# Thirty-two modulation sums on VectorE, moved behind the steps of a layer norm

## The chip, the core and the metric

The kernel runs on one core of a Trainium2 chip. The metric is device time in microseconds (us) for one execution. All times and rows here are of the kernel before.

The engines are TensorE (PE, with its weight loads PEld), VectorE (DVE), ScalarE (ACT), GpSimd (POOL) and SyncE (SP), which issues all DMAs of this kernel. Each engine works through its own instructions in a fixed order; an instruction that must wait holds up all that stands behind it on its engine.

## What is computed

One layer of a streaming encoder over 1024 tokens of width 1024, in float32. Cut to what matters here:

```python
mod = silu(c) @ w_ada + b_ada                     # 6 x 1024 numbers, one set for all tokens
shift1, scale1, gate1, shift2, scale2, gate2 = split(mod, 6)
h = rms_norm(x, norm1_g) * (1 + scale1) + shift1
z = h @ w_in                                      # query latent | key/value latent | rope key | conv | gates
q = rms_norm(z_q, ...) @ w_uq                     # attention branch
kv = rms_norm(z_kv, ...) @ w_ukv
u = causal_depthwise_conv(glu(z_glu), ...)        # convolution branch, 512 channels
u = silu(layer_norm(u, conv_ln_g, conv_ln_b))
x = x + gate1 * ((g_a * y_a + g_b * y_b) @ w_out)
x = x + gate2 * (relu((rms_norm(x) * (1 + scale2) + shift2) @ w_ff1) ** 2 @ w_ff2)
```

Of `mod`, the first third (shift1, scale1) is needed at once. The other 4 x 1024 numbers (gate1, shift2, scale2, gate2) are needed only after the attention.

## The kernel before

**Numbers in pairs.** A float32 matrix product is made of three products of rounded halves: `split` writes a rounded copy `hi` on ScalarE (L110) and the remainder `lo` on VectorE or GpSimd (L116). Names that end in hi/h and lo/l are such halves.

**The modulation sums.** One sum (`ada`, L276) multiplies a 128 x 1024 tile `wada` of w_ada by silu(c) and adds up each row: 128 numbers of `mod`, one column. It is two rows in a trace (the product and the reading of the accumulator). Sixteen sums belong to shift1 and scale1 and are done at the start. The 32 later ones, S1 to S32 in what follows, fill `mods`. Their tiles are loaded by SyncE (L271) into six buffers in turn, so the load for S7 waits until S1 has been done.

**The stretch of the change.** TensorE multiplies h by w_in, one 128-column tile after another, 48 products of 128x512 for a tile (`z` in the rows; `gate`, `z_tile`). Each tile writes two of four PSUM banks, which ScalarE (or VectorE) has to read out before a later tile may use them. The weights of a tile are loaded into `wraw` (L131), then split: `whi` on ScalarE, `wlo` on GpSimd. In order: ten gate tiles, the query latent in two tiles (`zr0`, `zr1`), the key/value latent (`zr2`), gate tile 10, the rope key (`zkr`), gate tiles 11 and 12. Beside this VectorE, ScalarE and GpSimd make the depthwise convolution (`conv`, L440 to L459) and then its layer norm (L488 to L514):

- `lnsum`: the four channel tiles `acc0` to `acc3` are added; split into `sh`, `sl`; TensorE adds up over channels with a column of ones (16 products of 128x2, "the statistics"); VectorE makes the mean `mu`; TensorE spreads it over the partitions by transposes (`spread`, L235); VectorE subtracts it (L498).
- `lnvar`: ScalarE squares, VectorE adds the squares (L504), again `sh`, `sl`, statistics, then 1/sqrt (`rln`, through a square root on ScalarE, L211), the spread and the products (L509).
- `sg`: a sigmoid on ScalarE (L511), gain and offset on GpSimd (L512), the last product on VectorE (L513), and a store to `cd` (L514). The tiles are read back much later.

Then comes the norm of the query latent (`latent_norm`, L592): squares of `zr0`, `zr1` into `lsq` and `lsq1` on ScalarE (L595, L598), sums of them on VectorE (L599), halves `lsh`, `lsl`, statistics on TensorE, `rl`, its spread, `zr` (L609), halves `zh`, `zl`. The same again for the key/value latent. `lsq` lies where the layer norm's `acc` tiles lay, so it waits for their stores.

**What sets the order.** The program is written step by step; the framework arranges the instructions of every engine by its own estimate of when each could run. `tc.issue_after(x)` only says that what stands in its block comes behind x on x's engine. Before the change all 32 sums stand in one such block behind `after`, the last instruction of the convolution, and are written behind the whole layer norm (L515). In the trace they run from 209 us to 275 us, between the steps of the layer norm.

Of the kernel before, what the change touches and what calls it, by code (L numbers as in the profile page):

```python
# [8 lines left out]
F32 = mybir.dt.float32  # L9
# [3 lines left out]
ALU = mybir.AluOpType  # L13
# [6 lines left out]
P = 128  # L20
C = 512
KD = D // P
# [55 lines left out]
def block_kernel(ctx: ExitStack, tc: tile.TileContext, a: dict, out: bass.AP):  # L78
# [23 lines left out]
    def cs(c):  # L102
        return slice(c * C, (c + 1) * C)
# [9 lines left out]

    def split(hi, lo, src, hi_eng, lo_eng):
        copy(hi_eng, hi, src)
        lo_eng.tensor_tensor(lo, src, hi.bitcast(F32), ALU.subtract)  # L116

    def mm(o, l, r, start, stop):
        nc.tensor.matmul(o, l, r, start=start, stop=stop)  # L119
# [79 lines left out]
    def stat_cols(src_hi, src_lo, blocks, off=0, st=None):  # L199

        st = bank("c") if st is None else st
        for b in range(blocks):
            o = st[:, 2 * b:2 * b + 2]
            mm(o, src_hi[:, blk(off + b)], ones, True, False)
            mm(o, src_lo[:, blk(off + b)], ones, False, True)
        return st[:, 0:2 * blocks].rearrange("p (b two) -> p b two", two=2)[:, :, 0]
# [10 lines left out]
    def rsqrt(pool, ssq, n, shape, name):  # L217

        ms = pool.tile(shape, F32, name=name + "_ms", bufs=1)
        r = pool.tile(shape, F32, name=name, bufs=1)  # L220
        t = pool.tile(shape, F32, name=name + "_t", bufs=1)
        nc.vector.tensor_scalar(ms, ssq, 1.0 / n, EPS, ALU.mult, ALU.add)
        last_rsqrt[0] = refined(r, ms, t)
        return r

    def spread(col, outs=None):

        return spread_rows(lambda t: col[:, t:t + 1].broadcast_to([P, P]), col.shape[1], outs)
# [187 lines left out]
    with tc.tile_pool(name="cv", bufs=1, **right) as cv:  # L416
        accs = [cv.tile([P, S], F32, name=f"acc{i}") for i in range(KC)]

        def tmp(name, dt=F32):
            return cv.tile([P, S], dt, name=name, tag="tmp", bufs=5)  # L420
# [57 lines left out]
        phase.close()  # L478
        phase.enter_context(psum(z=4, c=2, q=2))

        def sum_cols(src):
            sh_ = tmp("sh", F32R)
            sl_ = tmp("sl", F32R)
            for c in range(2):
                split(sh_[:, cs(c)], sl_[:, cs(c)], src[:, cs(c)], nc.scalar, nc.vector)
            return stat_cols(sh_, sl_, NB)

        s_ = tmp("lnsum")  # L488
        nc.gpsimd.tensor_tensor(s_, accs[0], accs[1], ALU.add)
        nc.vector.tensor_tensor(s_, s_, accs[2], ALU.add)  # L490
        nc.vector.tensor_tensor(s_, s_, accs[3], ALU.add)
        mu = cv.tile([P, NB], F32, name="mu")
        nc.vector.tensor_scalar(mu, sum_cols(s_), 1.0 / CH, None, ALU.mult)
        rb = spread(mu)
        vs = tmp("lnvar")
        for i in range(KC):
            for c in range(2):
# [3 lines left out]
            else:  # L501
                sq = tmp("lnsq")
                nc.scalar.activation(sq, accs[i], AF.Square)
                nc.vector.tensor_tensor(vs, vs, sq, ALU.add)  # L504
        r = rsqrt(cv, sum_cols(vs), CH, [P, NB], "rln")
        rb = spread(r)
        for i in range(KC):
            for c in range(2):
                nc.vector.tensor_tensor(accs[i][:, cs(c)], accs[i][:, cs(c)], rb[c], ALU.mult)  # L509
            sg = tmp("sg")  # L510
            nc.scalar.activation(sg, accs[i], AF.Sigmoid, scale=v("ln_g", i), bias=v("ln_b", i))  # L511
            nc.gpsimd.tensor_scalar(accs[i], accs[i], v("ln_g", i), v("ln_b", i), ALU.mult, ALU.add)  # L512
            nc.vector.tensor_tensor(accs[i], accs[i], sg, ALU.mult)  # L513
            nc.sync.dma_start(c_d[i], accs[i])  # L514
        with tc.issue_after(after.ins):  # L515
            for i in range(2, 6):
                for k in range(KD):
                    ada(mods[i - 2][:, k:k + 1], i * KD + k)
        nc.vector.scalar_tensor_tensor(amp2, scale2, 1.0, v("g2", 0, KD), ALU.add, ALU.mult)
        adap.close()  # L520

# [796 lines left out]
```

## Time and profile before

| | |
|---|---|
| median of 3 runs | 1380.77 us (1376.42 to 1384.38) |
| profiled execution | 1386.99 us |
| its span | 1385.2 us, mean granted clock of TensorE 0.988 |
| PE busy | 1325.0 us (96%) |
| DVE busy | 992.1 us (72%) |
| ACT busy | 686.0 us (50%) |
| POOL busy | 415.7 us (30%) |

How to read it: the span runs from the first to the last instruction of the profiled execution. That execution is 6.2 us longer than the median. TensorE is busy nearly throughout, so a wait on another engine matters only where TensorE then has nothing to do, or where its granted clock falls.

### The profile page before, as it was taken

To read this page: it belongs to the slowest core of one execution; us is meant where nothing else is said; L and a number is where in the kernel's file an instruction comes from. 1 tells how busy PE (TensorE), PEld (TensorE's weight loads), DVE (VectorE), ACT (ScalarE), POOL (GpSimd) and SP (SyncE) were. 2 spreads that over 40 slices of the span, in tenths; PEclk is the share of its full clock that TensorE was granted. 3 is DMA by queue.
4 is the path that set the end of the run, shared out by engine and by line. 5 is a ranking of instruction groups with operands and counts; after the bars stand their busy time and mean duration, and the time that the engine had idled before them with its cause. 6 is when DMAs were issued, how large, how long until landed. Compare 5 with 4: busy or idle time off the path is not lost.

```text
span 1385.2 us, 17860 instructions
## 1 busy us (share of the span) xinstructions
PE 1325.0 (96%) x6104; PEld 1079.5 (78%) x6104; DVE 992.1 (72%) x1526; ACT 686.0 (50%) x1115; POOL 415.7 (30%) x289
## 2 busy tenths in 40 slices
PE   4999999999999999999999999998999999999998
PEld 3787888777777888877787888876888888887787
DVE  6679997954347888877556899777773469857854
ACT  6545412245657777753354864434454444443343
POOL 0069822243566676435000004333433000000000
PEclk9999999999999999999999999999999999999999
DMA  9601227631285333137636565665557678633442
GB/s 345 238 31 61 92 99 288 251 109 71 85 296 204 104 120 102 69 119 231 188 131 220 175 228 198 206 210 186 194 185 256 207 229 289 200 95 92 146 128 76
DMA packets 105115, 233.93 MB, mean 169 GB/s; under 512 B 12352, under 2 KB 12608, under 8 KB 105024
## 3 DMA queue, kind: packets, MB, share of 16 engines
q1 hardware_dynamic: 105024, 232.79, 49.9%
q8 instruction: 48, 0.79, 0.2%
q14 instruction: 43, 0.35, 0.1%
HBM read 169.83 MB, written 62.91 MB: 168 GB/s over the span
## 4 chain that ended last, share of the span: by engine, by line
PE 61%; DVE 14%; DMA 10%; issue 5%; ACT 4%; POOL 4%; SPq 1%; DVEq 0%; POOLq 0%; ACTq 0%
PE z L119 49%; PE s L119 3%; DMA wraw<-in_w_ff 3%; PE t L119 3%; POOL accp L450 2%; PE v L119 2%; PE t L799 2%; DVE wada L276 1%; DMA gat<-sg 1%; DVE big L998 1%; DMA wada<-in_w_ada 1%; DVE u L1028 1%; DVE wlo L116 1%; PE x L119 1%; DVE wraw L999 1%
## 5 line engine op out<-in xcount | busy, mean ns | idle before, releaser
L119 PE MATMUL z<-hhi,whi 128*128 128x512 f32 x384 | 153.1, 399 | 2.9 <-ACT sg L406 2.9
L119 PE MATMUL z<-hhi,wlo 128*128 128x512 f32 x384 | 152.3, 398 | 1.5 <-POOL wlo L116 1.5
L119 PE MATMUL z<-hlo,whi 128*128 128x512 f32 x384 | 152.6, 397 | 0.0
L1053 POOL TENSOR_TENSOR t<-u 128x512 f32<-128x512 f32 x16 | 21.6, 1348 | 298.2 <-DVE wy L986 171.4
L457 DVE SCALAR_TENSOR_TENSOR k<-u,vec,k 128x1024 f32<-128x1024 f32 x84 | 101.0, 1283 | 0.0
L110 ACT ACTIVATE whi<-wraw 128x1024 fp32r<-128x1024 f32 x71 | 74.4, 1048 | 41.4 <-PE z L119 33.9
L116 POOL TENSOR_TENSOR wlo<-wraw,whi 128x1024 fp32r<-128x1024 f32 (+1 forms) x23 | 56.1, 2440 | 122.8 <-ACT whi L110 122.8
L119 PEld LDWEIGHTS z<-hhi,whi 128*128 128x128 f32 x384 | 72.6, 189 | 21.5 <-ACT sg L406 3.5
L119 PEld LDWEIGHTS z<-hhi,wlo 128*128 128x128 f32 x384 | 72.4, 189 | 19.8 <-POOL wlo L116 1.9
L119 PEld LDWEIGHTS z<-hlo,whi 128*128 128x128 f32 x384 | 72.6, 189 | 17.8
L1019 ACT ACTIVATE u<-u 128x512 f32<-128x512 f32 x64 | 40.1, 631 | 85.4 <-DVE u L1028 81.7
L116 DVE TENSOR_TENSOR wlo<-wraw,whi 128x1024 fp32r<-128x1024 f32 x48 | 63.4, 1321 | 24.6 <-ACT whi L110 24.5
L276 DVE CUSTOM_DVE_ANT_0 wada<-wada,c_act,vec 128x1024 f32<-128x1024 f32 x48 | 68.0, 1455 | 10.6 <-DMA wada<-in_w_ada 7.3
L1028 DVE TENSOR_TENSOR u<-z,u 128x512 f32<-128x512 f32 x80 | 53.9, 686 | 23.5 <-DMA fdT<-u 11.2
L450 POOL TENSOR_TENSOR accp<-accp,prc 128x1024 f32<-128x1024 f32 x28 | 69.3, 2479 | 1.4
L119 PE MATMUL z<-ghT,hi 128*128 128x512 f32 x160 | 62.7, 392 | 0.3 <-DVE u L1028 0.3
L119 PE MATMUL z<-ghT,lo 128*128 128x512 f32 x160 | 62.5, 391 | 0.0
L119 PE MATMUL z<-glT,hi 128*128 128x512 f32 x160 | 62.4, 390 | 0.0
L119 PE MATMUL z<-l_whi,h_whi 128*128 128x512 f32 x148 | 58.8, 398 | 3.2 <-DVE l_whi L116 3.2
L119 PE MATMUL z<-l_wraw,h_wraw 128*128 128x512 f32 x152 | 59.6, 392 | 0.0
L119 PE MATMUL z<-h_wraw,l_wraw 128*128 128x512 f32 x152 | 59.2, 389 | 0.0
L119 PE MATMUL z<-h_whi,l_whi 128*128 128x512 f32 x148 | 58.6, 396 | 0.0
(365 smaller groups left out, 3859.6 us busy)
## 6 DMA issues: line engine op xcount, KB each, us to landing
wada<-in_w_ada SPq DMA_DIRECT2D x48, 512.0 KB, 6.2
wraw<-in_w_ff SPq DMA_DIRECT2D x32, 512.0 KB, 4.4
fraw<-fdT SPq DMA_DIRECT2D x64, 256.0 KB, 2.6
wraw<-in_w_in SPq DMA_DIRECT2D x24, 512.0 KB, 3.6
fd<-u SPq DMA_DIRECT2D x48, 256.0 KB, 3.4
fdT<-t SPq DMA_DIRECT2D x48, 256.0 KB, 4.1
fraw<-fd SPq DMA_DIRECT2D x48, 256.0 KB, 2.7
w<-in_w_ff SPq DMA_DIRECT2D x48, 256.0 KB, 3.8
```

What stands on the lines that cost most here:

```text
L110: eng.activation(o, i, AF.Copy)
L116: lo_eng.tensor_tensor(lo, src, hi.bitcast(F32), ALU.subtract)
L119: nc.tensor.matmul(o, l, r, start=start, stop=stop)
L276: nc.vector.tensor_tensor_reduce(out=w, in0=w, in1=c_act, scale=1.0, scalar=v("b_ada", j), op0=ALU.mult, op1=ALU.add, accum_out=dst,)
L450: nc.gpsimd.tensor_tensor(accp, accp, pr, ALU.add)
L457: nc.vector.scalar_tensor_tensor(t, u[:, j:j + S], w(j), t, ALU.mult, ALU.add)
L799: nc.tensor.transpose(pt[:, blk(n)], probs[q - i + 1][:, blk(kb)], ident)
L998: nc.vector.tensor_tensor(q[:, cs(0)], p[:, cs(0)], q[:, cs(0)], ALU.subtract)
L999: nc.vector.tensor_tensor(p[:, cs(1)], p[:, cs(1)], y[:, cs(1)], ALU.subtract)
L1019: nc.scalar.activation(f, f, AF.Relu)
L1028: last_sum[0] = nc.vector.tensor_tensor(t, x, y, ALU.add)
L1053: nc.gpsimd.tensor_tensor(t3, f22, f12, ALU.subtract)
```

## The change

The 32 sums are no longer in one block. A list `others` holds them; `more(n, step)` takes the next n and writes them behind the instruction `step`, and `split` now returns its last instruction so that it can serve as one. One sum stands behind the convolution, 3 behind the `sl` of the mean, 2 behind `mu`, 2 behind the `sl` of the variance, 1 behind the 1/sqrt, 2 behind the last product with it, and the other 21 behind the layer norm's last product. Nothing that is computed changes.

```diff
-        lo_eng.tensor_tensor(lo, src, hi.bitcast(F32), ALU.subtract)
+        return lo_eng.tensor_tensor(lo, src, hi.bitcast(F32), ALU.subtract)
...
+        others = [(i, k) for i in range(2, 6) for k in range(KD)]
+
+        def more(n, step):
+            with tc.issue_after(step.ins):
+                for _ in range(min(n, len(others))):
+                    i, k = others.pop(0)
+                    ada(mods[i - 2][:, k:k + 1], i * KD + k)
...
-            return stat_cols(sh_, sl_, NB)
+            st = stat_cols(sh_, sl_, NB)
+            more(n, o)
+            return st
...
+        more(1, after)
...
-        nc.vector.tensor_scalar(mu, sum_cols(s_), 1.0 / CH, None, ALU.mult)
+        o = nc.vector.tensor_scalar(mu, sum_cols(s_, 3), 1.0 / CH, None, ALU.mult)
         rb = spread(mu)
+        more(2, o)
...
-        r = rsqrt(cv, sum_cols(vs), CH, [P, NB], "rln")
+        r = rsqrt(cv, sum_cols(vs, 2), CH, [P, NB], "rln")
         rb = spread(r)
+        more(1, last_rsqrt[0])
...
+            if i == KC - 1:
+                more(2, o)
...
-        with tc.issue_after(after.ins):
-            for i in range(2, 6):
-                for k in range(KD):
-                    ada(mods[i - 2][:, k:k + 1], i * KD + k)
+        more(len(others), o)
```

How many of the 32 sums stand ahead of a step in VectorE's order, and what lies between the steps in TensorE's order:

| step on VectorE | sums ahead, before | now | on TensorE | before | now |
|---|---|---|---|---|---|
| last addition of `lnsum` | 6 | 1 | products of the gate tiles ahead of the mean's statistics | same place | same place |
| first subtraction of the mean | 21 | 6 | products from the mean's statistics to its spread | 20 | 19 |
| last addition of `lnvar` | 31 | 6 | from that spread to the variance's statistics | 115 | 63 |
| first product with `rln` | 32 | 9 | from those to the spread of `rln` (and 4 or 2 inside them) | 26 | 26 |
| last product of the layer norm | 32 | 11 | from there to the first statistic of the query latent | 98 | 120 |
| first addition of `lsq` | 32 | 17 | | | |
| `lsl` of the query latent | 32 | 20 | | | |
| `zr` of the query latent | 32 | 28 | | | |

The orders of the engines differ from the mean's spread up to the first part of the attention (some 250 to 500 us in the trace), and are the same behind it.

VectorE at the variance, before: the additions of the squares with sums between them (`mod5` is the last column group, gate2).

```order
L504 TENSOR_TENSOR lnvar_1820<-lnvar_1820,lnsq_1831 128x1024
L276 ISA wada_1993,mod5_78<-wada_1993,c_act_102,vec_63 128x1024
L276 ISA mod5_78 128x1
L276 ISA wada_1996,mod5_78<-wada_1996,c_act_102,vec_63 128x1024
L276 ISA mod5_78 128x1
L276 ISA wada_1999,mod5_78<-wada_1999,c_act_102,vec_63 128x1024
L276 ISA mod5_78 128x1
L504 TENSOR_TENSOR lnvar_1820<-lnvar_1820,lnsq_1836 128x1024
```

VectorE at the variance, now:

```order
L517 TENSOR_TENSOR lnvar_1838<-lnvar_1838,lnsq_1844 128x1024
L517 TENSOR_TENSOR lnvar_1838<-lnvar_1838,lnsq_1849 128x1024
L517 TENSOR_TENSOR lnvar_1838<-lnvar_1838,lnsq_1854 128x1024
L116 TENSOR_TENSOR sl_1858<-lnvar_1838,sh_1857 128x512 x2
L276 ISA wada_1880,mod2_75<-wada_1880,c_act_102,vec_63 128x1024
```

The additions and `sl` now stand in a row; the next sum (S7) comes behind them.

VectorE at the norm of the query latent, before: nothing stands between its steps.

```order
L513 TENSOR_TENSOR acc3_690<-acc3_690,sg_1904 128x1024
L599 TENSOR_TENSOR lsq_2144<-lsq_2144,lsq1_2146 128x512
L599 TENSOR_TENSOR lsq_2144<-lsq_2144,lsq1_2150 128x512
L116 TENSOR_TENSOR lsl_2154<-lsq_2144,lsh_2153 128x512 x2
L222 TENSOR_SCALAR rl_ms_2176<-c_2159 128x8
```

The same place now, from the first addition on; ahead of it, behind the layer norm's last product, stand S12 to S17.

```order
L612 TENSOR_TENSOR lsq_2144<-lsq_2144,lsq1_2146 128x512
L276 ISA wada_1960,mod4_77<-wada_1960,c_act_102,vec_63 128x1024
L276 ISA mod4_77 128x1
L612 TENSOR_TENSOR lsq_2144<-lsq_2144,lsq1_2150 128x512
L276 ISA wada_1963,mod4_77<-wada_1963,c_act_102,vec_63 128x1024
L276 ISA mod4_77 128x1
L276 ISA wada_1966,mod4_77<-wada_1966,c_act_102,vec_63 128x1024
L276 ISA mod4_77 128x1
L116 TENSOR_TENSOR lsl_2154<-lsq_2144,lsh_2153 128x512 x2
```

Nine sums have come ahead of `lsl`, three of them between its own steps.

ScalarE behind the query latent's 1/sqrt, before (`sg_2528` and `sg_2531` read gate tile 11 out of its banks, `zh0` and `zh1` are halves of the query latent, `lsq_2269` the squares of the key/value latent):

```order
L211 ACTIVATE rl_2177<-rl_ms_2176 128x8
L406 ACT_TABLE_LOAD
L406 ACTIVATE sg_2528<-z_2478 128x512
L110 ACTIVATE whi_2536<-wraw_2534 128x1024
L406 ACTIVATE sg_2531<-z_2479 128x512
L110 ACTIVATE zh0_2195<-zr0_2025 128x512
```

ScalarE at the same place now:

```order
L211 ACTIVATE rl_2177<-rl_ms_2176 128x8
L110 ACTIVATE zh0_2195<-zr0_2025 128x512
L110 ACTIVATE zh1_2203<-zr1_2026 128x512
L110 ACTIVATE zh0_2195<-zr0_2025 128x512
L608 ACTIVATE lsq_2269<-zr2_2027 128x512 x2
L110 ACTIVATE zh1_2203<-zr1_2026 128x512
L406 ACT_TABLE_LOAD
L406 ACTIVATE sg_2528<-z_2478 128x512
```

The halves and the squares have come ahead of the sigmoid of gate tile 11. A second change of this kind stands at the end of the key/value latent's norm: there `whi`, a table load and a sigmoid of gate tile 12 have come between the square root and the halves `zh2`.

## Rows read from the trace of the kernel before

**Rows 1.** The page: busy time of the first engine, and the chain by engine.

```profile
PE 1325.0 (96%) x6104; PEld 1079.5 (78%) x6104; DVE 992.1 (72%) x1526; ACT 686.0 (50%) x1115; POOL 415.7 (30%) x289
PE 61%; DVE 14%; DMA 10%; issue 5%; ACT 4%; POOL 4%; SPq 1%; DVEq 0%; POOLq 0%; ACTq 0%
```

**Rows 2.** Windows: stretch, length, busy PE, PEld, DVE, ACT, POOL, clock, DMA.

```profile
270.00:275.00 5.00, 4.41 (x20) 3.24 (x19) 5.00 (x10) 1.35 (x3) 0.00 (x0) 1.00 0.29 100
275.00:280.00 5.00, 5.00 (x26) 4.13 (x25) 1.88 (x7) 2.89 (x5) 0.00 (x0) 0.75 0.01 3
280.00:285.00 5.00, 5.00 (x22) 3.99 (x21) 0.00 (x0) 1.83 (x3) 2.39 (x1) 0.91 0.21 72
335.00:340.00 5.00, 3.24 (x10) 2.36 (x11) 3.34 (x8) 1.87 (x4) 0.49 (x1) 0.55 0.37 114
340.00:345.00 5.00, 5.00 (x18) 3.93 (x17) 1.65 (x4) 2.57 (x6) 3.32 (x2) 0.76 0.00 0
```

**Rows 3.** Timeline of PE: start, length, instruction, count, idle before it and releaser.

```profile
272.86 0.40 PE L119 MATMUL z<-hhi,whi 128*128 128x512 f32 x1
273.09 0.40 PE L119 MATMUL z<-hlo,whi 128*128 128x512 f32 x1
274.31 0.27 PE L119 MATMUL c<-ones,sh 128*128 128x2 f32 x1 [0.59 <-ACT sh L110]
...
305.79 0.49 PE L119 MATMUL z<-hhi,whi 128*128 128x512 f32 x1 [2.41 <-ACT sg L406]
...
318.86 1.03 PE L235 MATMUL c<-ident,rl 128*128 128x128 f32 x8
...
336.05 1.94 PE L235 MATMUL c<-ident,rl 128*128 128x128 f32 x8 [1.63 <-DVE rl L215]
338.64 2.50 PE L119 MATMUL z<-zh,whi 128*128 128x512 f32 x4 [0.65 <-ACT zh L110]
```

**Rows 4.** Timeline of DVE: layer norm, sums between, then the query latent.

```profile
248.90 2.47 DVE L498 TENSOR_TENSOR acc<-acc,c 128x512 f32<-128x512 f32 x4
...
264.28 1.27 DVE L276 CUSTOM_DVE_ANT_0 wada<-wada,c_act,vec 128x1024 f32<-128x1024 f32 x1
265.49 1.21 DVE L504 TENSOR_TENSOR lnvar<-lnvar,lnsq 128x1024 f32<-128x1024 f32 x1
266.62 3.42 DVE L276 CUSTOM_DVE_ANT_0 wada<-wada,c_act,vec 128x1024 f32<-128x1024 f32 x1
...
272.38 1.22 DVE L504 TENSOR_TENSOR lnvar<-lnvar,lnsq 128x1024 f32<-128x1024 f32 x1
...
319.50 2.72 DVE L609 SCALAR_TENSOR_TENSOR zr<-zr,vec,c 128x512 f32<-128x512 f32 x4 [4.66 <-PE c L235]
```

**Rows 5.** Timeline of POOL: two of the weight splits.

```profile
265.61 3.34 POOL L116 TENSOR_TENSOR wlo<-wraw,whi 128x1024 fp32r<-128x1024 f32 x1 [3.63 <-ACT whi L110]
...
280.14 2.39 POOL L116 TENSOR_TENSOR wlo<-wraw,whi 128x1024 fp32r<-128x1024 f32 x1 [11.19 <-ACT whi L110]
```

**Rows 6.** The chain of waits at the layer norm's end: start, length, what.

```profile
285.49 3.09 DVE acc L509 x5
...
295.72 4.59 DVE acc L513
...
300.33 2.63 DMA cd<-acc
```

**Rows 7.** Timeline of ACT from the layer norm's end to the key/value latent's norm.

```profile
303.07 0.63 ACT L595 ACTIVATE lsq<-zr 128x512 f32<-128x512 f32 x1 [8.86 <-DMA cd<-acc]
...
318.39 1.28 ACT L406 ACT_TABLE_LOAD   x1 [4.39 <-PE z L119]
319.69 0.60 ACT L406 ACTIVATE sg<-z 128x512 f32<-128x512 f32 x1
...
321.61 1.68 ACT L110 ACTIVATE zh<-zr 128x512 fp32r<-128x512 f32 x3
...
331.99 1.06 ACT L110 ACTIVATE whi<-wraw 128x1024 fp32r<-128x1024 f32 x1 [0.15 <-PE z L119]
```

More of the change, by code (lines that the diff above doesn't have):

```diff
@@ L479, in block_kernel, with sum_cols @@
         phase.enter_context(psum(z=4, c=2, q=2))
-        def sum_cols(src):
+        others = [(i, k) for i in range(2, 6) for k in range(KD)]
[4 more added lines that the diff above has]
+                    ada(mods[i - 2][:, k:k + 1], i * KD + k)
+        def sum_cols(src, n):
             sh_ = tmp("sh", F32R)
@@ L484, in sum_cols @@
             for c in range(2):
-                split(sh_[:, cs(c)], sl_[:, cs(c)], src[:, cs(c)], nc.scalar, nc.vector)
-            return stat_cols(sh_, sl_, NB)
+                o = split(sh_[:, cs(c)], sl_[:, cs(c)], src[:, cs(c)], nc.scalar, nc.vector)
+            st = stat_cols(sh_, sl_, NB)
+            more(n, o)
+            return st
         s_ = tmp("lnsum")
         nc.gpsimd.tensor_tensor(s_, accs[0], accs[1], ALU.add)
+        more(1, after)
         nc.vector.tensor_tensor(s_, s_, accs[2], ALU.add)
@@ L504, in block_kernel @@
                 nc.vector.tensor_tensor(vs, vs, sq, ALU.add)
-        r = rsqrt(cv, sum_cols(vs), CH, [P, NB], "rln")
+        r = rsqrt(cv, sum_cols(vs, 2), CH, [P, NB], "rln")
         rb = spread(r)
+        more(1, last_rsqrt[0])
         for i in range(KC):
             for c in range(2):
-                nc.vector.tensor_tensor(accs[i][:, cs(c)], accs[i][:, cs(c)], rb[c], ALU.mult)
+                o = nc.vector.tensor_tensor(accs[i][:, cs(c)], accs[i][:, cs(c)], rb[c], ALU.mult)
+            if i == KC - 1:
+                more(2, o)
             sg = tmp("sg")
@@ L512, in block_kernel @@
             nc.gpsimd.tensor_scalar(accs[i], accs[i], v("ln_g", i), v("ln_b", i), ALU.mult, ALU.add)
-            nc.vector.tensor_tensor(accs[i], accs[i], sg, ALU.mult)
+            o = nc.vector.tensor_tensor(accs[i], accs[i], sg, ALU.mult)
             nc.sync.dma_start(c_d[i], accs[i])
-        with tc.issue_after(after.ins):
-            for i in range(2, 6):
-                for k in range(KD):
-                    ada(mods[i - 2][:, k:k + 1], i * KD + k)
+        more(len(others), o)
         nc.vector.scalar_tensor_tensor(amp2, scale2, 1.0, v("g2", 0, KD), ALU.add, ALU.mult)
```

## The prediction, made before the changed kernel was run

> **What bounds the kernel now.** I read the page first: TensorE is busy in 96% of the span, and the chain that ended last runs through it for 61% [rows 1]. So a change on VectorE can give back only what TensorE loses beside the sums and shortly behind them. The windows of five microseconds show where that is [rows 2]. In the stretch from 209 to 345 us TensorE loses time at three places: around 274 us it is idle for a moment, and its granted clock then falls to 0.75 and 0.91 in two windows; at 303 us it waits; and between 334 and 345 us it waits again and shows 0.55 and 0.76. The granted clock is a mean of two levels, 1.2 and 2.4 GHz, so 0.55 is a window nearly all at the lower one. The timeline of TensorE names the waits [rows 3]: 0.59 us for the variance's `sh`; 2.41 us, at 305.79, for the sigmoid that empties the banks of gate tile 10; then 1.63 and 0.65 us at the norm of the key/value latent.
>
> All that TensorE loses there adds up as follows. Waits: 0.59 + 2.41 + 1.63 + 0.65 = 5.3 us. Slow clock at 275 to 285: 5 x 0.25 + 5 x 0.09 = 1.7. Slow clock at 335 to 345: 5 x 0.45 + 5 x 0.24 = 3.45, less 0.8 for the 1.76 us in which TensorE was idle anyway: 2.65. Sum **9.6 us**. That is the most that the change can win in this stretch.
>
> **What the change does to the layer norm.** The mean's part gains nothing: its statistics stand at the same place of TensorE's order, and TensorE sets when that place is reached. The variance is another matter. Before, the three additions of squares stand with six sums between them, and two of them lie 6.9 us apart (265.49 and 272.38) [rows 4]. Now they stand in a row, and TensorE's order has the statistics 52 products earlier. Products follow one another at 0.23 us (272.86, 273.09) [rows 3], so TensorE gets there 52 x 0.23 = 12.0 us earlier than the 273.7 at which it began to wait (274.31 less 0.59): at 261.7. VectorE is in time: even if the subtraction starts no earlier than 248.90, eight halves take 2 x 2.47, three additions 3 x 1.21, `sl` about 1.3, which ends at 258.8 [rows 4]; a weight split on GpSimd may hold it for 2.4 more, 261.2. So the 0.59 us wait goes, and I take the slow clock behind it (1.7) as gone too.
>
> From the statistics to the spread of 1/sqrt there are 26 products in either order, so the products with it start some 14.3 us earlier than 285.49 [rows 6]: 12.6 from the earlier place and the saved wait, 1.7 from the clock. Behind them something is given back: two sums (2.4) stand ahead of the last products, and a table load of 1.28 (the length in [rows 7]) may now have to wait for VectorE. So the end of the layer norm comes 10.6 to 14.3 us earlier. Its last product, 301.5 before (300.31 and 1.2 for the fourth), is then at 287.2 to 290.9; the third store, whose landing let ScalarE begin with `lsq` at 303.07 [rows 6, 7], lands in time for a start at 289 to 292.5. Gate tile 10's sigmoid stands right behind, and its banks are asked for by gate tile 11 only 48 products (11 us) after tile 10 ends, near 290. So the **2.41 us wait goes** as well.
>
> **What takes its place.** The 21 other sums must still run, 1.21 us from one to the next (264.28 to 265.49) [rows 4], and they now stand in the queue in which the query latent's norm stands. Three places follow from the order.
>
> (1) `lsl`. TensorE: spread done at 271.7, 120 products and ten more, 29.9: it wants `lsl` at 301.6. VectorE: last product of the layer norm at 287.2 to 290.9, nine sums 10.9, two additions and the first half of `lsl` 1.8: 299.9 to 303.6. GpSimd's weight splits come on top. In the trace a sum that met one took 3.42 us, not 1.27 (266.62), while the split, alone 2.39, took 3.34 behind an addition (265.61) [rows 4, 5]: they do not overlap, whoever came second waits. Of two splits in question none to both fall here, 0 to 4.8. So the wait is 0 to 6.8 us. One split, that of gate tile 11, is certain to meet the sums, because its `whi` follows gate tile 10's end; with it and the middle of the range, 301.75 + 2.4, I take **2.6**.
>
> (2) The sigmoid of gate tile 11. Gate tile 12 needs those banks. ScalarE now makes the latent's halves and two squares first. From the start of the spread: `zr` begins after 0.64 (318.86 to 319.50) and takes 2.72 for four [rows 3, 4]; `zh` at 0.56 each, the squares 0.55 each, the table load 1.28 and the sigmoid 0.60 end at about 6.9 [rows 7]. TensorE has 1.03 of spread and 17 products, 4.9: it waits 2.0. Besides, S21 to S28 stand between `lsl` and `zr`: 9.7 us, with the rest of `lsl` and `rl` 11.1, where TensorE takes 9.4 for statistics and 31 products. That is 1.7 more, or 4.1 more if a split is met. So 2.0 to 6.1; I take **3.7**, since the split of gate tile 12 is due about when `lsl` is.
>
> (3) The key/value latent's halves. Between the square root and `zh2` ScalarE has a weight split that waits for gate tile 12's last product (1.06), a table load (1.28) and a sigmoid (0.60); with `zh2` 3.5, of which the spread hides 1.03 [rows 3, 7]: **2.5**. The waits of 1.63 and 0.65 before are replaced by this one.
>
> (4) The clock. A fall cost 1.7 and 2.65 in the trace, and not every pause brings one: behind the 2.41 us no window is below 1.00. Three pauses of 2 to 4 us can bring none or two falls, 0 to 5.3; I take one, **2.2**.
>
> SyncE's queue moves too: each later load waits for a sum, and weight loads stand between. At the tightest place, the weights of gate tile 12, the load stands behind the third store (about 288 to 290), takes 2.6 us for as many bytes [rows 6] or somewhat more, and ScalarE cannot split them before the rope key's tile ends, beyond 301. I price it at nothing; if the queue were held 10 us longer, TensorE would wait for it.
>
> Sum: 2.6 + 3.7 + 2.5 + 2.2 = 11.0 us of new losses for 9.6 of old ones, **+1.4 us**. With the low ends (0, 2.0, 2.5, 0) it is -5.1, with the high ends (6.8, 6.1, 2.5, 5.3) +11.1. The profiled execution took 1386.99 us, 1.8 more than its span of 1385.2; the median of the runs is 6.2 below it, and I apply the difference to the median: 1380.77 + 1.4, **1382.2 us**. Later changes in the order, up to the attention, I leave at nothing, some 2 us to either side.
>
> The Trainium skill ("GPSIMD Engine Reference", Key points) says that GpSimd shares its interfaces to SBUF with VectorE and contends with VectorE instructions that have two SBUF inputs; the sums are such. The 3.42 us row agrees. By this rule every sum that meets a split counts as in (1) and (2); were it not so, (1) would be nearer 0.2 and the total near -1.
>
> **The rivals.** *All gain, no loss.* The sums behind the layer norm slip into gaps of VectorE (in 280 to 285 us it shows 0.00 busy [rows 2]), loads and splits fall well, and the new order fits. Then up to 9.6 us are won: 1371. For it: VectorE's work here is less than the time. Against it: it is one queue, and nine sums stand ahead of a step on which TensorE waits. To be faster by over 0.5% (6.9 us) the new losses must stay under 2.7.
>
> *The sums behind the layer norm hold the latents' norms.* This is the mechanism of (1) and (2) at their high ends: the layer norm ends at 291, both splits fall among the sums, TensorE waits 6.8 and 6.1 us, and the clock falls twice. Then 1391.9. It decides for slower once the new losses pass 9.6, and for more than 0.5% once they pass 16.5.
>
> *The layer norm ends no earlier*, because a load of sums holds SyncE and the weights come late: then the 21 sums begin at 301 and the latents' norms come up to 10.9 later (nine sums): 1391 or so.
>
> **How the numbers follow.** 0.5% is about what a measurement of this kernel can tell from no change. The forecast, 1373.9 to 1387.7, has 0.66. All gain has 0.16. Slower has 0.18: 0.15 for the held norms, 0.03 for the late layer norm. The range for 8 in 10 reaches down to the first rival's 1371 and up to the second's, about 1391.
>
> **What would show it.** Right: the variance's statistics near 262 us without a wait; the windows at 275 to 285 with a clock of 1.00; `lsq` on ScalarE at 289 to 293; no wait of 2.4 us at gate tile 11; in its place waits of TensorE for `lsl`, for the sigmoid of gate tile 11 and for `zh2`, 2 to 4 us each; sums of 3.4 us beside weight splits. The products with `zh2`, at 338.64 before, would start within 3 us of that. Wrong: `zh2` reached before 332, or beyond 345; a long wait for a weight load; or a difference that arises behind 345 us.

## The result, and the profile after

The changed kernel took 1391.1 us (median of 8 runs, 1387.94 to 1394.69), the kernel before 1380.38 in the same measurement (8 runs). The ratio is 1.0072, with a 95% interval of 1.0050 to 1.0093: slower by 0.7%, at the upper end of the predicted range and not in the forecast case (1382.2 us, no change to within 0.5%). Its profiled execution took 1391.5 us, so it is a typical one. The profiled execution of before lies 6.6 us above its median, so the pair of traces shows only 4.5 of the 10.7 us.

The page of the changed kernel, busy time and chain [rows 1]:

```profile
PE 1326.3 (95%) x6104; PEld 1082.3 (78%) x6104; DVE 990.2 (71%) x1526; ACT 685.9 (49%) x1115; POOL 416.8 (30%) x289
PE 62%; DVE 14%; DMA 9%; issue 5%; ACT 4%; POOL 4%; SPq 1%; DVEq 0%; ACTq 0%; POOLq 0%
```

TensorE (PE) has 1.3 us more busy time, and the chain is nearly the same. The place has to be looked for in the stretch of the change. The windows there, columns as in [rows 2]:

```profile
275.00:280.00 5.00, 5.00 (x23) 4.05 (x22) 4.04 (x6) 5.00 (x5) 3.66 (x2) 1.00 0.43 141
280.00:285.00 5.00, 5.00 (x24) 4.00 (x22) 2.50 (x2) 1.54 (x3) 5.00 (x3) 1.00 0.69 279
...
305.00:310.00 5.00, 3.50 (x12) 3.11 (x13) 5.00 (x8) 0.00 (x0) 0.90 (x1) 0.62 1.00 399
310.00:315.00 5.00, 5.00 (x17) 3.95 (x16) 4.86 (x15) 0.21 (x1) 0.00 (x0) 0.70 0.92 330
...
340.00:345.00 5.00, 3.08 (x10) 2.26 (x11) 2.65 (x5) 3.64 (x6) 3.45 (x2) 0.87 0.52 157
345.00:350.00 5.00, 5.00 (x19) 3.90 (x18) 1.12 (x2) 4.20 (x9) 3.36 (x3) 0.79 0.00 0
```

The slow clock at 275 to 285 is gone, 1.00 in both windows. In its place stand 0.62 and 0.70 at 305 to 315, which is 5 x 0.38 + 5 x 0.30 = 3.4 us, and 0.87 and 0.79 at 340 to 350, 1.7 us (in both, time in which TensorE was idle anyway is counted in). TensorE's timeline names the waits ahead of them, columns as in [rows 3]:

```profile
261.58 0.17 PE L119 MATMUL c<-ones,sh 128*128 128x2 f32 x1
...
299.59 0.27 PE L119 MATMUL c<-ones,lsh 128*128 128x2 f32 x1 [0.66 <-ACT lsh L110]
...
303.75 0.27 PE L119 MATMUL c<-ones,lsl 128*128 128x2 f32 x1 [1.46 <-DVE lsl L116]
...
306.50 0.37 PE L119 MATMUL c<-ones,lsl 128*128 128x2 f32 x1 [1.70 <-DVE lsl L116]
...
324.50 0.50 PE L119 MATMUL z<-hhi,whi 128*128 128x512 f32 x1 [1.90 <-ACT sg L406]
...
341.90 1.49 PE L119 MATMUL z<-zh,whi 128*128 128x512 f32 x4 [2.51 <-ACT zh L110]
```

The variance's statistics start at 261.58 without a wait. Then come waits in the query latent's norm (0.66 + 1.46 + 1.70 = 3.8), for the sigmoid of gate tile 11 (1.90) and for `zh2` (2.51). VectorE shows why `lsl` is late (compare [rows 4]):

```profile
270.54 4.87 DVE L523 TENSOR_TENSOR acc<-acc,c 128x512 f32<-128x512 f32 x8 [4.16 <-PE c L235]
...
285.48 3.42 DVE L529 TENSOR_TENSOR acc<-acc,sg 128x1024 f32<-128x1024 f32 x1 [0.94 <-POOL acc L528]
...
291.23 3.41 DVE L276 CUSTOM_DVE_ANT_0 wada<-wada,c_act,vec 128x1024 f32<-128x1024 f32 x1
...
303.01 3.43 DVE L116 TENSOR_TENSOR lsl<-lsq,lsh 128x512 fp32r<-128x512 f32 x2
```

The products with `rln` start at 270.54 instead of 285.49, and the layer norm ends at 288.9: its last product takes 3.42 us, beside a weight split that began on GpSimd at 285.42. Then the sums follow, one of them 3.41 us long. The last row is the two halves of `lsl`: the first takes 0.68, the second 2.83. Two more weight splits (compare [rows 5]) stand beside that sum and that second half:

```profile
291.05 2.50 POOL L116 TENSOR_TENSOR wlo<-wraw,whi 128x1024 fp32r<-128x1024 f32 x1 [3.24 <-ACT whi L110]
303.28 2.62 POOL L116 TENSOR_TENSOR wlo<-wraw,whi 128x1024 fp32r<-128x1024 f32 x1 [9.72 <-ACT whi L110]
```

ScalarE (compare [rows 7]) begins with `lsq` at 287.27, and has the split, the table load and the sigmoid of gate tile 12 ahead of `zh2`:

```profile
287.27 0.64 ACT L608 ACTIVATE lsq<-zr 128x512 f32<-128x512 f32 x1 [5.72 <-DMA cd<-acc]
...
338.37 1.06 ACT L110 ACTIVATE whi<-wraw 128x1024 fp32r<-128x1024 f32 x1 [1.29 <-PE z L119]
339.44 1.28 ACT L406 ACT_TABLE_LOAD   x1
340.73 0.60 ACT L406 ACTIVATE sg<-z 128x512 f32<-128x512 f32 x1
341.23 1.14 ACT L110 ACTIVATE zh<-zr 128x512 fp32r<-128x512 f32 x2
```

All this is worth 3.3 us by the first product with `zh2` (341.90 against 338.64 in [rows 3]). The other losses had to be found by stage.

### The profile page after: what moved, and what is told of

It is laid out like the page before. It is cut to its first block, busy times and chain, and to the rows that moved or that the text cites. A ratio compares the mean times of both kernels' runs of the same rounds, so it can differ in the third digit from the quotient of the medians.

```text
span 1389.7 us, 17850 instructions
## 1 busy us (share of the span) xinstructions
PE 1326.3 (95%) x6104; PEld 1082.3 (78%) x6104; DVE 990.2 (71%) x1526; ACT 685.9 (49%) x1115; POOL 416.8 (30%) x289
## 4 chain that ended last, share of the span: by engine, by line
PE 62%; DVE 14%; DMA 9%; issue 5%; ACT 4%; POOL 4%; SPq 1%; DVEq 0%; ACTq 0%; POOLq 0%
PE z L119 51%; DMA wraw<-in_w_ff 3%; PE s L119 3%; POOL accp L450 2%; PE t L119 2%; PE v L119 2%; DMA gat<-sg 1%; PE t L812 1%; DVE wada L276 1%; DVE u L1041 1%; DVE big L1011 1%; DVE wlo L116 1%; DVE wraw L1012 1%; PE x L119 1%; DMA big<-in_w_ff 1%
## 5 line engine op out<-in xcount | busy, mean ns | idle before, releaser
L1032 ACT ACTIVATE u<-u 128x512 f32<-128x512 f32 x64 | 40.1, 630 | 79.7 <-DVE u L1041 76.1
L276 DVE CUSTOM_DVE_ANT_0 wada<-wada,c_act,vec 128x1024 f32<-128x1024 f32 x48 | 65.1, 1391 | 3.2 <-ACT c_act L110 3.2
L119 PE MATMUL z<-l_wlo,h_wlo 128*128 128x512 f32 x148 | 57.8, 390 | 0.1
```

The lines of the kernel that those rows point to most:

```text
L276: nc.vector.tensor_tensor_reduce(out=w, in0=w, in1=c_act, scale=1.0, scalar=v("b_ada", j), op0=ALU.mult, op1=ALU.add, accum_out=dst,)
L1032: nc.scalar.activation(f, f, AF.Relu)
```

## Experiments: where the 10.7 us are

I cut each trace at three places of TensorE's timeline: the first product with `zh2` (key/value latent), the transposes of `rows` for the queries' norm (c<-ident,rows, the start of the attention), and the first product with `ahi` (a rounded half of the attention's output, its end). Such transposes stand twice in each trace; those of the keys' norm come some 50 us earlier and are not meant, also where an expectation says "the first transposes of rows". Every kernel has the same number of products in each stage (1372, 348, 1096 and 3288), so no work has moved from one stage to another. Behind the attention all kernels have nearly the same order. All rows are from one profiled execution each, which can lie several us off the kernel's median (rest_free 7.3 above, no_rest 6.0); "sums" gives the groups in the order of the change, and behind a plus the rest. The attention comes in two orders: A, that of before, and B, that of the changed kernel.

| kernel | sums | order | zh2 | zh2 to rows | rows to ahi | ahi to end | ratio to before (95%) |
|---|---|---|---|---|---|---|---|
| before | - | A | 338.6 | 79.6 | 187.9 | 779.1 | |
| before_again | - | A | 337.2 | 79.7 | 187.4 | 774.4 | |
| changed kernel | 1,3,2,2,1,2 + 21 | B | 341.9 | 81.7 | 192.9 | 773.3 | 1.0072 (1.0050 to 1.0093) |
| after_again | the same | B | 340.6 | 79.6 | 192.6 | 775.0 | |
| rest_free | 1,3,2,2,1,2, 21 free | B | 354.9 | 79.8 | 193.1 | 777.2 | 1.0129 (1.0094 to 1.0163) |
| no_rest | 1,3,2,2,1,2, 21 left out | B | 329.4 | 81.7 | 192.8 | 778.1 | 0.9963 (0.9939 to 0.9988) |
| all_behind | 0,0,0,0,0,0 + 32 | B | 348.9 | 79.6 | 191.4 | 774.3 | 1.0139 (1.0102 to 1.0175) |
| balanced | 1,13,3,4,3,3 + 5 | A | 332.2 | 86.8 | 188.9 | 772.0 | 1.0017 (0.9995 to 1.0038) |
| balanced_b | 1,13,3,4,4,4 + 3 | B | 337.3 | 82.7 | 192.0 | 772.2 | 1.0040 (1.0023 to 1.0056) |
| early | 5,12,3,4,3,3 + 2 | A | 332.3 | 87.8 | 188.1 | 773.8 | 1.0021 (1.0000 to 1.0041) |
| four_last | 1,3,2,2,1,4 + 19 | A | 342.5 | 85.7 | 187.4 | 777.8 | 1.0088 (1.0060 to 1.0116) |
| six_a | 1,10,3,3,1,6 + 8 | A | 340.3 | 79.6 | 187.9 | 775.8 | 1.0060 (1.0037 to 1.0082) |
| six_b | 1,13,2,3,1,6 + 6 | B | 339.5 | 78.7 | 193.5 | 771.4 | 1.0036 (1.0021 to 1.0051) |
| before_tq | as before | B | 334.8 | 80.9 | 193.2 | 773.0 | 1.0040 (1.0020 to 1.0060) |

### Second executions

The kernel before once more, without an edit:

> The kernel before, unchanged, for a second profiled execution. Three theories on the loss of 10.7 us. *Held norms*: the sums behind the layer norm make TensorE wait in the latents' norms, 3.8 + 1.9 + 2.5 us, and its clock falls there (3.4 + 1.7). *Later order*: the other order behind 345 us costs the most. *Low base*: the profiled execution of before was itself 6.6 us above its median, because the clock happened to fall at 275 to 285 and 335 to 345 us, so what I counted as won there (9.6 us) is in part not there in most executions. Held norms and later order expect the same picture again: waits of 0.59, 2.41, 1.63 and 0.65 us and windows of the clock below 1.00 at 275 to 285 and 335 to 345, time 1380 to 1387. Low base expects the same waits within 0.5 us, but at least one of the two falls of the clock missing, and a time of 1377 to 1382.

It took 1380.42 us. Windows, columns as in [rows 2]:

```profile
275.00:280.00 5.00, 4.40 (x25) 3.45 (x24) 3.33 (x9) 2.68 (x5) 0.00 (x0) 0.90 0.01 3
280.00:285.00 5.00, 5.00 (x18) 3.95 (x18) 0.24 (x2) 3.39 (x4) 2.39 (x1) 0.76 0.00 0
...
335.00:340.00 5.00, 3.86 (x14) 2.89 (x15) 2.76 (x4) 2.21 (x3) 1.17 (x1) 0.70 0.31 108
340.00:345.00 5.00, 5.00 (x22) 3.94 (x22) 1.98 (x3) 3.82 (x8) 3.09 (x3) 0.96 0.00 0
```

Both falls are there again, the second at half the size: 1.7 us, or 1.4 without the time in which TensorE was idle, as the prediction counts it. The wait of 2.41 us at gate tile 11 is missing; those of 0.60, 1.63 and 1.06 (for `zh2`) are there. So the old losses of this execution are 3.3 + 1.7 + 1.4 = 6.4 us, not 9.6. (A wait of 0.44 us for the sigmoid of gate tile 11 stands in both executions and is in neither sum.) The sign that "low base" named, a missing fall, did not come, but its point holds for some 3 us of the sum, though by `zh2` the two executions are only 1.4 us apart. Most of the 6.6 us between them arose behind the attention (779.1 against 774.4), where TensorE's order is the same.

The changed kernel once more:

> The changed kernel, unchanged, for a second profiled execution. Two orders of the attention: the same three stages as in its first profile, to within 1.5 us each: zh2 at 342, 82 us from there to the transposes of rows, 193 us from those to the first product with ahi; waits for lsl, the sigmoid of gate tile 11 and zh2 within 0.5 us of the first. What differs from the first execution is falls of the clock elsewhere; 1387 to 1395. Held norms alone: the stage at the attention may shrink to 188 us.

1389.65 us. The waits agree (0.67, 1.45, 1.70, 1.91, 2.52), and so does the stage of the attention, 192.6. The stage ahead of it was 79.6 and not 82. Over the two executions of either kernel the changed one loses 3.4 us up to `zh2`, 1.0 up to the attention and 5.1 in it: 9.5 together. The 1.0 is not shown: the changed kernel's 81.7 and 79.6 reach down to before's 79.6 and 79.7.

### The sums behind the layer norm

Part of the change undone, the rest of the sums bound to the convolution's end again:

```diff
-        more(len(others), o)
+        more(len(others), after)
```

> The changed kernel, but the 21 other sums are bound only to the convolution's last instruction, as all 32 were before; the scheduler then puts all 32 ahead of the first addition of lsq, none between the latents' steps. TensorE's order is that of the changed kernel but for 1081 to 1543 of its 5376 rows (from the variance's statistics to the last gate tile, about 255 to 365 us), and the same behind. Held norms: the waits for lsl, for the sigmoid of gate tile 11 and for zh2 go (8.2 us) and most of the slow clock with them; 1371 to 1381, ratio to before 0.993 to 1.000. Later order: the loss stays but for 1 to 3 us, since behind 365 us the order is that of the changed kernel; 1386 to 1390, ratio 1.004 to 1.007. Low base: what the changed kernel won was small, so with the waits gone it comes out level with before, 1378 to 1383, ratio 0.998 to 1.002.

All three missed: 1399.53 us. The loss stands ahead of `zh2` (354.9). TensorE's timeline and VectorE's:

```profile
318.89 0.79 PE L119 MATMUL z<-hhi,whi 128*128 128x512 f32 x1 [10.68 <-ACT sg L406]
```

```profile
281.16 0.16 DVE L215 SCALAR_TENSOR_TENSOR rln<-rln_t,rln 128x8 f32<-128x8 f32 x1
...
287.68 2.61 DVE L276 CUSTOM_DVE_ANT_0 wada<-wada,c_act,vec 128x1024 f32<-128x1024 f32 x1 [2.74 <-DMA wada<-in_w_ada]
290.21 4.86 DVE L523 TENSOR_TENSOR acc<-acc,c 128x512 f32<-128x512 f32 x8
```

Eleven sums now stand between the variance's `sl` and the products with `rln`; one of them also waits 2.74 us for its tile. The products come at 290.21, later than before (285.49). On ScalarE the sigmoid that empties TensorE's banks stands behind `lsq`, and `lsq` waits for the layer norm's stores until 316.17; so TensorE waits 10.68 us for that sigmoid. The waits for `lsl` are gone. So the sums cost at a step of the layer norm as well, not only in the latents.

The 21 sums left out:

```diff
+    for m in mods:
+        nc.gpsimd.memset(m, 0.5)
...
-        more(len(others), o)
```

> The changed kernel without the 21 sums behind the layer norm and without their loads (modulation columns filled with 0.5 instead: that part is left out). It is the most that any place for them can win. Held norms: 1370 to 1378, ratio 0.992 to 0.998, no wait for lsl, and at most 1 us for the sigmoid of gate tile 11. Later order: 1383 to 1388, ratio 1.002 to 1.005, since the order behind 365 us is that of the changed kernel. Low base: 1375 to 1381, ratio 0.996 to 1.000.

1378.03 us. The time fits "held norms" and "low base" about equally well; the waits decide. From 200 us up to 329.4 TensorE has none above 0.1 us, so the 21 sums with their loads cost 341.3 - 329.4 = 12 us by `zh2` (mean of the changed kernel's two executions): held norms, as expected. The sums were not separated from their loads. The attention takes 192.8 here as well, though. So the 5 us there are not a consequence of the held norms.

All 32 behind the end:

```diff
-        more(1, after)
...
-        o = nc.vector.tensor_scalar(mu, sum_cols(s_, 3), 1.0 / CH, None, ALU.mult)
+        o = nc.vector.tensor_scalar(mu, sum_cols(s_, 0), 1.0 / CH, None, ALU.mult)
...
-        more(2, o)
...
-        r = rsqrt(cv, sum_cols(vs, 2), CH, [P, NB], "rln")
+        r = rsqrt(cv, sum_cols(vs, 0), CH, [P, NB], "rln")
...
-        more(1, last_rsqrt[0])
...
-            if i == KC - 1:
-                more(2, o)
```

> All 32 sums behind the layer norm's last product, none between its steps: the part of the change that places 11 in groups is undone, and the part that puts the rest behind the end is taken further. 6 stand ahead of the first addition of lsq, 9 ahead of lsl, 18 ahead of the first zr and 27 to 32 at the key/value latent; the attention has an order of the changed kernel's kind. Held norms: the wait for lsl and the sigmoid as in the changed kernel, and VectorE still has sums to do at the key/value latent, so that zl and kn come late too; zh2 at 342 to 350 us (341.9 in the changed kernel), 1390 to 1397, ratio 1.007 to 1.012. If the groups inside the layer norm were what cost the time, it would come out at 1380 to 1386.

1399.89 us, with `zh2` at 348.9 as expected: the groups inside the layer norm don't cost, they save 7.6 us up to there (348.9 against 341.3). Time and ratio are a little above what was expected.

### Other group sizes

The first of these runs changes only the sizes, and so do the others of this part (table):

```diff
-        o = nc.vector.tensor_scalar(mu, sum_cols(s_, 3), 1.0 / CH, None, ALU.mult)
+        o = nc.vector.tensor_scalar(mu, sum_cols(s_, 13), 1.0 / CH, None, ALU.mult)
...
-        more(2, o)
+        more(3, o)
...
-        r = rsqrt(cv, sum_cols(vs, 2), CH, [P, NB], "rln")
+        r = rsqrt(cv, sum_cols(vs, 4), CH, [P, NB], "rln")
...
-        more(1, last_rsqrt[0])
+        more(3, last_rsqrt[0])
...
-                more(2, o)
+                more(3, o)
```

> The changed kernel with other group sizes: 1, 13, 3, 4, 3, 3 and the last 5 behind the end, instead of 1, 3, 2, 2, 1, 2 and 21. VectorE has nothing to do from about 226 to 241 us, while TensorE makes the mean's statistics and spread; the 13 fill that. All 32 then stand ahead of the first addition of lsq, and TensorE's order is that of the run with the 21 sums set free. Held norms: both the early layer norm and the undisturbed latents, 1371 to 1379, ratio 0.993 to 0.999. Later order: 1386 to 1390, ratio 1.004 to 1.007. Low base: 1376 to 1382, ratio 0.997 to 1.001.


1383.98 us, level with before, and between the theories' ranges. One statement of the expectation is wrong: from the last gate tile on, the order of the engines is that of before (A), not that of the run with the sums set free. `zh2` comes 5 us earlier than in before's two executions, but only its first products do; the next ones wait for more of the halves:

```profile
335.55 0.73 PE L119 MATMUL z<-zh,whi 128*128 128x512 f32 x2 [1.92 <-ACT zh L110]
...
338.04 0.79 PE L119 MATMUL z<-zl,whi 128*128 128x512 f32 x1 [1.29 <-DVE zl L116]
```

So part of the gain is only the place of the cut. With these waits, one of 2.30 us for `sqh` (a half of the queries' squares; 0.65 before) and 3.2 us more of slow clock, the stage takes 86.8 us instead of 79.6.

> The changed kernel with 4 instead of 2 sums behind the last product with rln, so 19 instead of 21 behind the layer norm's end. In the latents the sums still stand between the steps (20 ahead of the second addition of lsq, 25 ahead of rl, 30 ahead of the last zr). But from the first heads of the attention on, the order of TensorE, ScalarE, VectorE and GpSimd is that of before, not that of the changed kernel. *Two orders of the attention* (my theory after the first runs: of the loss of 10.7 us about 4 arise at the latents up to the first product with zh2, about 2 up to the attention, and about 5 in the attention, whose order has changed): attention 188 us long from the first transposes of rows to the first product with ahi, and 1384 to 1388, ratio 1.003 to 1.006. *Held norms alone* (the 5 us in the attention follow from what the norms cost, not from the order): attention 193 us, time as the changed kernel's, 1389 to 1393, ratio 1.006 to 1.009.

The attention took 187.4 us, as expected from its order A; the time did not follow: 1394.13 us, because the stage ahead of it took 85.7. TensorE's and ScalarE's timelines there:

```profile
413.06 0.59 PE L119 MATMUL q<-sqh,sel 128*8 128x512 f32 x1 [5.44 <-ACT sqh L630]
```

```profile
411.92 0.60 ACT L629 ACTIVATE sqf<-z 128x512 f32<-128x512 f32 x1 [6.78 <-DMA qd<-qf]
```

The wait hangs on a store of the queries (`qd`), by this view; what held it was not tried.

> Groups of 1, 13, 3, 4, 4, 4 and the last 3, against 1, 13, 3, 4, 3, 3 and 5 of the run called balanced. The latents are nearly the same, all 32 sums ahead of the first addition of lsq; but the attention now has the order of the changed kernel. Two orders of the attention: the time from the first transposes of rows to the first product with ahi is 193 us instead of the 189 of balanced, with a second fall of the clock some 22 us behind its start; 1386 to 1391, ratio 1.004 to 1.008. Held norms alone: as balanced or, with two sums fewer behind the end, up to 2 us less, 1381 to 1385, ratio 1.000 to 1.003.

192.0 us in the attention and 1386.45 us: both as "two orders" has it. By the ratios, balanced with order A is 0.0040 - 0.0017 of 1381 us, 3.2 us, shorter in total; but the two intervals overlap, so this pair alone does not show it.

> Groups of 5, 12, 3, 4, 3, 3 and only 2 behind the end: VectorE's second idle stretch, 212 to 219 us, gets four sums too. Orders from lsq on as in balanced, with the attention of before. Two orders of the attention and held norms both expect a little less than balanced: the wait for lsh (0.44 us at 300) and the fall of the clock behind it (1.7) go, 1380 to 1383, ratio 0.999 to 1.002. If five sums ahead of the mean's sl make its statistics late, TensorE waits at 240 us and it is 1383 to 1388.

1383.63 us, a little above what was expected and no better than balanced. The wait for `lsh` stayed (0.37 us), only the fall of the clock behind it went, and a wait of 1.37 us for a weight split (`wlo`, at 292.15) is new. TensorE does not wait at 240 us, so the mean's statistics were not late.

> Groups of 1, 10, 3, 3, 1, 6 and the last 8 behind the layer norm's end. 14 sums stand ahead of the variance, 30 ahead of the first addition of lsq, all 32 ahead of lsl. Unlike the changed kernel it has before's order on every engine from the end of the latents' norms on, in the attention too. Two orders of the attention: 188 us from the first transposes of rows to the first product with ahi, 79 to 81 us from zh2 to those transposes (before 79.6), and the early layer norm without held norms; zh2 at 330 to 338 us, 1373 to 1381, ratio 0.995 to 1.000. Held norms alone expects the same here. If sums in the layer norm's own steps cost as much as sums in the latents' norms, zh2 comes beyond 340 and it is 1384 to 1390.

The time was missed: 1387.66 us, `zh2` at 340.3. SyncE's queue (start, length, issue), and ScalarE:

```profile
293.14 0.33 SPq L131 DMA_DIRECT2D wraw<-in_w_in  x1
293.56 0.38 SPq L271 DMA_DIRECT2D wada<-in_w_ada  x1
294.04 2.40 SPq L530 DMA_DIRECT2D cd<-acc  x4
```

```profile
303.20 0.64 ACT L608 ACTIVATE lsq<-zr 128x512 f32<-128x512 f32 x1 [10.79 <-DMA cd<-acc]
```

Three of the four tiles were done by 289.9, but all four stores went out at 294.04, behind a load of weights issued at 293.14. Its buffer was most likely held by the weight split on GpSimd, which ran from 290.76 to 293.12, behind the layer norm's last offset. So `lsq` began at 303.20, no earlier than before [rows 7], and TensorE waited 1.76 us for the sigmoid behind it, and 1.20 for that split. In the changed kernel three stores went out from 280.01 on. The Trainium skill ("DMA: Bandwidth & Descriptors", Anatomy of one DMA — SWDGE (gpsimd) path) says that DMA engines do not wait on semaphores and that any such wait happens on the issuing sequencer before dispatch; its section is on DMAs that GpSimd issues, and these rows, of SyncE's queue, agree.

> Groups of 1, 13, 2, 3, 1, 6 and the last 6: the partner of six_a, with three sums more behind the mean's sl and one fewer behind mu. The norms of the layer norm and the latents stand as in six_a (TensorE's first product of the latent's statistics at the same row, the same order up to the attention but for single rows), only the attention has the changed kernel's order. Two orders of the attention: 192 to 193 us from the first transposes of rows to the first product with ahi, so 4 to 5 us longer than six_a: ratio to six_a 1.003 to 1.004, 1378 to 1386. Held norms alone: level with six_a, within 2 us.

The attention's stage was as expected, 193.5 us against 187.9, but the total was not: 1385.47 us, below six_a. In the profiled pair six_b is 4.4 us shorter behind the attention, where the order is nearly the same; that is within what this stage varies by (771.4 to 779.1 in the table). The intervals of the two ratios overlap, too. This pair doesn't show the 5 us in the total.

### The switch of the attention's order

Up to here seven traces with order B have 191.4 to 193.5 us in the attention, and six with order A 187.4 to 188.9. SyncE's queue shows the first difference. Before, then the changed kernel:

```profile
423.63 0.33 SPq L534 DMA_DIRECT2D t_q<-in_rope_q  x1
428.97 0.33 SPq L735 DMA_DIRECT2D mb<-mbt  x1
430.46 1.09 SPq L559 DMA_DIRECT2D qkf<-kd  x2
```

```profile
433.92 0.32 SPq L748 DMA_DIRECT2D mb<-mbt  x1
434.34 0.92 SPq L547 DMA_DIRECT2D t_q<-in_rope_q  x1
...
436.79 1.09 SPq L572 DMA_DIRECT2D qkf<-kd  x2
```

`t_q` is a table of 512 KB for the rotation of the queries, `mb` a product of the convolution's output, which VectorE has to make first, `kd` the keys of the second head. Before, the table is issued 5.3 us ahead of the store. Now it stands behind it, and close ahead of the keys. From the keys' issue to the start of ScalarE's work on them pass 3.3 us before and 4.4 in the changed kernel, and ScalarE waits longer for them. Before, then the changed kernel:

```profile
433.72 0.63 ACT L110 ACTIVATE khi<-qkf 128x512 fp32r<-128x512 f32 x1 [1.82 <-DMA qkf<-kd]
```

```profile
441.21 0.63 ACT L110 ACTIVATE khi<-qkf 128x512 fp32r<-128x512 f32 x1 [3.41 <-DMA qkf<-kd]
```

This wait is 1.63 to 1.90 us in the six traces with order A and 2.99 to 3.80 in the seven with B. TensorE then waits for an exponential (`pr`):

```profile
445.35 0.39 PE L119 MATMUL s<-khi,qhi 128*128 128x256 f32 x1 [1.16 <-ACT pr L789]
```

The second 20 us of the attention, TensorE alone (busy, granted clock, DMA share and GB/s), before and changed:

```profile
438.20:458.20 20.00, 18.51 (x122) 1.00 0.52 166
```

```profile
443.60:463.60 20.00, 17.39 (x96) 0.91 0.38 122
```

Behind the wait the clock falls once more: (1 - 0.91) x 20 us is 1.8 lost, and 1.1 us less is busy. That is 2.9 of the 5 us; another 1.7 in the changed kernel is a fall of the clock some 180 us into the stage, in both its executions and in neither of before's. Over the whole stage TensorE is idle for 10.8 to 11.3 us in the six traces with order A and 12.2 to 13.4 in the seven with B. Slow clock takes 3.4 us in each of the six and 5.1 to 6.8 in the seven, not always at the same place.

To test it I took the kernel before and moved nothing but this load:

```diff
-                    nc.sync.dma_start(mb_d[d][:, cs(c)], t)
+                    mb_store[0] = nc.sync.dma_start(mb_d[d][:, cs(c)], t)
...
-        pools.update(att=att, odd=odd, t_q=rotation(odd))
+        with tc.issue_after(mb_store[0].ins):
+            pools.update(att=att, odd=odd, t_q=rotation(odd))
```

With that the framework gives the attention order B (on TensorE, ScalarE and GpSimd row for row, on VectorE and SyncE but for a few rows), and leaves all ahead of it as it was.

> The kernel before with one edit: the load of the query's rotation table (t_q) on SyncE is bound behind the store of the first product of the convolution's output (mb). The 32 sums, the layer norm and the latents are those of before, in before's order; the attention then has the changed kernel's order on all engines, the only thing of the change that is in it. Cause in SyncE's queue (my theory now): in the seven profiles with this order the load of the second head's keys (kd), which stands behind t_q, comes late: ScalarE waits 3.0 to 3.8 us for it instead of 1.6 to 1.9, TensorE then 1.16 us for the exponentials, and the clock falls a second time. So here too: a wait of 3.0 to 3.8 us for kd, 192 to 193 us from the first transposes of rows to the first product with ahi (before 187.4 and 187.9), and 1383 to 1387, ratio 1.002 to 1.005. Rival: the five us in the attention come with what the sums do ahead of it (memory traffic, late loads), and the order only goes along: then the stage stays at 188 us and the time within 0.15% of before.

1386.8 us against 1381.66, ratio 1.0040 (1.0020 to 1.0060), and 193.2 us in the attention. SyncE, ScalarE and TensorE:

```profile
426.46 0.32 SPq L735 DMA_DIRECT2D mb<-mbt  x1
426.89 0.37 SPq L534 DMA_DIRECT2D t_q<-in_rope_q  x1
427.95 1.09 SPq L559 DMA_DIRECT2D qkf<-kd  x2
```

```profile
432.50 0.63 ACT L110 ACTIVATE khi<-qkf 128x512 fp32r<-128x512 f32 x1 [3.11 <-DMA qkf<-kd]
435.02 0.63 ACT L110 ACTIVATE qhi<-qkf 128x512 fp32r<-128x512 f32 x1 [1.90 <-POOL qkf L555]
```

```profile
436.79 0.33 PE L119 MATMUL s<-khi,qhi 128*128 128x128 f32 x1 [1.19 <-ACT pr L778]
...
438.49 0.39 PE L119 MATMUL s<-khi,qhi 128*128 128x256 f32 x1 [1.16 <-ACT pr L778]
```

So the order alone, with all sums where they were, costs 0.4%, 5 us (0.2 to 0.6%, 3 to 8 us), and the rival, that the sums' work ahead of it costs them, falls. A second fall of the clock is not needed for it: there is one at this place (1.7 us), but the one at the stage's start is smaller by as much, and slow clock takes 3.4 us in all, as before. TensorE is idle for 14.6 us instead.

That the late keys are the cause is only what the waits suggest. The late table is a rival: GpSimd begins to work on it at 431.94, 16.2 us into the stage, and before at 430.41, 12.2 us into it; it multiplies the queries by it, and ScalarE waits 1.90 us for these queries right behind the keys. With the load's place the orders of all engines change, too, and none of this was tried one by one. Nor is it shown why the sums' new places make the framework turn the two DMAs; the runs only show which of them do.

Up to the attention this run is a third execution of before's order. It has no wait at gate tile 11 and reaches `zh2` at 334.8, so one order differs by some 4 us there (334.8 to 338.6), and the changed kernel's loss up to `zh2` is 3.4 us against two executions and 4.4 against all three. Its 80.9 us from there to the attention lie within the changed kernel's 79.6 to 81.7.

None of the kernels beats before but no_rest, which leaves work out.

## Why the prediction came out as it did

**The layer norm: right, but for one range.** The statistics were predicted at 261.7 without a wait and started at 261.58; the products 14.3 us earlier, and they came 14.95 earlier; the end at 287.2 to 290.9, and it was 288.9; `lsq` at 289 to 292.5, and it was 287.27, earlier than the range. The wait at gate tile 11 and the slow clock at 275 to 285 went; but the wait is missing in two of three executions of before's order as well, so that it went is not shown to be the change's doing.

**The new losses: right in kind, three of four mis-sized.** Mechanism (1), `lsl`: 3.8 us against 2.6, inside its 0 to 6.8. A part of it, 0.66, is a wait for `lsh`, which stands behind the same sums; the last 1.70 came from a split that met `lsl` itself. Three splits met steps of VectorE here, where the prediction counted with one of two. Mechanism (2), the sigmoid: 1.9 against 3.7, just below its low end of 2.0. ScalarE's order cost about what was said for it (2.0); the 1.7 for S21 to S28 did not come, as TensorE was late itself and reached the spread, at 317.60, without a wait. Mechanism (3), `zh2`: 2.51 against 2.5. Mechanism (4), the clock: two falls, 3.4 + 1.7 = 5.1, or 4.3 without TensorE's idle time, as the prediction counts it, against 2.2 and inside its 0 to 5.3. Sum 12.5 instead of 11.0.

**The old losses: too large for a typical execution.** 9.6 us were in the one trace; the second execution shows 6.4. The 2.41 us at gate tile 11 are there in one of three executions of the same order; what decides that was not tried.

**The step that failed** is one sentence: "Later changes in the order, up to the attention, I leave at nothing, some 2 us to either side." They cost 5.1 us in the attention (means of two executions, 192.75 against 187.65), because its order turned as a whole; up to it they cost 1.0, which is not shown. The sign that I named for being wrong, a difference that arises behind 345 us, is there. I had looked at the orders of VectorE, ScalarE and TensorE near the sums, and at SyncE's queue only for weights; that the orders differ into the first part of the attention was on record, but the turn of two DMAs there, 100 us behind the last sum, I had not priced. The other part is the size of the losses by `zh2`: 3.4 us instead of 1.4. The products with `zh2` stand 3.26 us later, just beyond the 3 us that were to show the prediction right. Together, 1380.4 + 3.4 + 1.0 + 5.1 = 1389.9, against 1391.1 measured.

Of the rivals, the held norms came true as a mechanism but not at their price (12.5 us of new losses, where 16.5 were needed for half a per cent). "All gain" fell with the waits for `lsl`. The layer norm did end earlier, so the third rival is out.

That the time still lies at the end of the range, about 1391, is luck. That end is the held norms' 1391.9, with the longest waits and both falls of the clock; what brought the time there are the 5 us of the attention, which neither the sum nor a rival had.

## What to carry to other kernels

Where a framework arranges the order by its own estimates, a local change can turn far-off pairs of instructions: compare every queue to its end, the DMA queue above all, and price each pair that has changed places by the waits that already stand behind it. Filler work on a queue that steps of a chain go through costs by where it meets such a step; it cost least in the stretch in which VectorE waits for TensorE anyway (13 sums there in balanced, and no wait for `lsl`). One profiled execution of the kernel before is a sample: a second one tells which of its losses are always there.

## What was not expected of the hardware

- Falls of the granted clock differ between executions of the same order. Before, what windows of 5 us below 0.97 lose while TensorE still works adds up to 16.1 us over the span in one execution and 13.7 in the other; at 335 to 345 us the fall took 3.4 us in one (idle time included) and 1.7 in the other. Behind the attention 14 executions took 771.4 to 779.1 us in nearly the same order.
- A 128x1024 instruction of VectorE with two tiles as inputs that meets a weight split on GpSimd took 3.41 and 3.42 us (291.23, 285.48), as in [rows 4], against 1.27 alone. A 128x512 one, the second half of `lsl`, took 2.83 against 0.68.
